# Seven half-size products from the fifth hidden block on, in a float32 SwiGLU FFN pair

## The chip, the cores and the metric

The kernel runs on one core of a Trainium2 chip. The metric is the device time of one execution in microseconds. The engines are named as the profile names them: PE is TensorE (PEld its weight loads), DVE is VectorE, ACT is ScalarE, POOL is GpSimd and SP is SyncE; the last two issue most of the DMA transfers here.

## The reference

One layer of a decoder: a half-step SwiGLU FFN, a token mixer (RWKV-7 heads beside differential attention), and a second half-step FFN, with an RMS norm before and after each. 512 prompt tokens and 8 × 4 sample tokens, 544 in all; model width 1024, hidden width 2816, all float32. The change touches the two FFNs alone.

```python
def swiglu(x, w_in, w_out):
    gate, up = jnp.split(x @ w_in, 2, axis=-1)
    return (jax.nn.silu(gate) * up) @ w_out

def layer(x, l, shift0, wkv0, attend, P):
    g = P['norm_gains'][l]
    h = x + 0.5 * rms_norm(swiglu(rms_norm(x, g[0], NORM_EPS), P['ff1_in'][l], P['ff1_out'][l]), g[1], NORM_EPS)
    m, k, v, wkv, shift = mixer(rms_norm(h, g[2], NORM_EPS), l, shift0, wkv0, attend, P)
    h = h + rms_norm(m, g[3], NORM_EPS)
    h = h + 0.5 * rms_norm(swiglu(rms_norm(h, g[4], NORM_EPS), P['ff2_in'][l], P['ff2_out'][l]), g[5], NORM_EPS)
    return h, k, v, wkv, shift
```

## The kernel before

**Layout.** Activations lie with the features on the 128 partitions and the tokens in the free dimension, in two halves s = 0, 1 of 272 tokens (`HALF`). The width of 1024 is 8 blocks of 128 (`KB`), the hidden width 22 blocks (`FB`).

**Float32 by parts.** Every factor of a matmul is split in two: a high part that ScalarE writes as a rounded copy (`whi`, `xh`, `hd0h`, `sh`), and a low part, the difference (`wlo`, `xl`, `hd0l`, `sl`). A product is three matmuls: high·high, high·low, low·high (L148, L149, L154). `weights` (L112) loads a block of weights, splits it, and makes the low either by a subtraction on VectorE (L124) or, with `added`, as a negated copy on ScalarE (L121) to which a GpSimd transfer adds the weights from memory while it moves them (L122).

**Two kinds of hidden blocks.** A whole block of an FFN multiplies the 8 feature blocks of both token halves with the gate and the up weights: 4 dot products of 24 matmuls, 96 in all. A mixed block, `seven`, takes gate and up as the two rows of a 2 × 2 product with the token halves as its columns, splits the 8 feature blocks in two halves of 4, and computes the four results from seven half-size products of 12 matmuls, 84 in all, with sums and differences before and after. Its left factors are made for each block in `load` and `factors` from the weights: `b` (`raw`, as it is), `b22`, `t1` and `t2`. `t1` is loaded twice from one place by SP (L469), and a GpSimd transfer then adds to it in place (L473); the low of `b` is a negated copy on ScalarE (L494) with an accumulating transfer (L495); `t2` is two additions of VectorE (L497, L498). Its right factors are made once for each FFN in `combined`: `scaled` scales h by the norm in place and splits three of the four quarters (16 steps: L417, and the parts `fa` at L406 on ScalarE and L408 or L410 on VectorE), and `mixtures` overwrites h with four sums or differences of its quarters, 4 tiles each (16 steps: L430, and the parts `sh` and `sl` at L406 and L408). When the last mixture is through, the memory of h is freed, and the pool `wt` with t1, b22 and their parts takes it (L469 and L471 wait for that).

**Groups.** `GROUPS` cuts the 22 blocks into four groups. After each, `products` multiplies the group's hidden tiles (`hd0`, `hd1`) with the output weights: 16 products (8 output blocks u × 2 halves), each of 3 matmuls a hidden block, over the weights of one u at a time. The first group's results are copied from PSUM by ScalarE (L615), those of later groups added by VectorE (L620). The first group is of whole blocks, all later ones of mixed blocks. `scaled` is run in pieces of four steps while blocks 4 and 5 are computed, and `mixtures` two steps with each result of the first group (in `finish`).

**Order.** Within these lines the order of each engine's instructions is set when the program is built, by a scheduler that uses the data's dependences, priorities and `after(...)`, which keeps instructions behind a given one. TensorE's hidden products and the output products of a group run one after the other; in later groups the next mixed block is begun before the output products.

## Time and profile before

| | us |
|---|---|
| median of 3 runs | 1195.4 (1192.81 to 1197.7) |
| profiled execution, its own time | 1202.05 |
| its span | 1200.3 |
| TensorE busy in the span | 1175.4 |
| VectorE busy | 823.3 |
| ScalarE busy | 583.7 |

The granted clock of TensorE was 0.986 over the span. FF1 lies in the first third of the span and FF2 in the last; the mixer stands between them. A line of the timeline reads: start in us from the span's start, duration, engine, line, operation, tile written, tiles read, shape, count, and in brackets the wait before it with what ended it. A matmul's duration there is its way through the pipeline; the pace shows in the starts.

### The profile page before, as it was taken

The page shows a single profiled execution, that of the slowest core. Times are in us where ns is not written, and L with a number is a line of the kernel's source. Part 1 is how long each engine was busy: PE and PEld are TensorE (multiplying, and loading weights), DVE is VectorE, ACT ScalarE, POOL GpSimd, SP SyncE. Part 2 cuts the span into 40 slices and gives each one's busy share as a digit, 9 for nine tenths or more (in the row PEclk, how much of TensorE's full clock was granted, in tenths as well). Part 3 has the DMA queues.
Part 4 walks back from the last instruction along what each step waited for, and adds up shares of the span by engine and source line. Part 5 has one row for each costly group of instructions (what it writes and reads, how often), then busy time and mean ns, then how long its engine had stood idle before and what let it go on. Part 6 is the DMA issues. An engine that isn't in the chain of part 4 may idle for free. (4 is left out here: it accounts for less than half of the span.)

```text
span 1200.3 us, 25442 instructions
## 1 busy us (share of the span) xinstructions
PE 1175.4 (98%) x10020; PEld 1109.7 (92%) x10020; DVE 823.3 (69%) x1878; ACT 583.7 (49%) x1081; POOL 170.9 (14%) x232
## 2 busy tenths in 40 slices
PE   8999999999999999999999999999999999999996
PEld 8999999999999999989887645999999999999995
DVE  7794684865875777768426657888784765857756
ACT  6455552643645664443114535666455634625530
POOL 0001210110101165531000031100002201101001
PEclk9999999999999998899899999999999999999998
DMA  7328885884857456789543468563349876957532
GB/s 257 110 68 239 218 211 122 205 197 120 184 174 201 118 147 182 223 218 256 131 141 104 142 245 297 162 184 124 101 119 243 210 186 152 216 145 183 116 121 75
DMA packets 85833, 205.42 MB, mean 171 GB/s; under 512 B 9144, under 2 KB 20152, under 8 KB 84306
## 3 DMA queue, kind: packets, MB, share of 16 engines
q1 hardware_dynamic: 65378, 148.64, 37.5%
q0 software_dynamic: 18032, 50.70, 23.5%
q10 hardware_dynamic: 2304, 4.46, 1.0%
q8 instruction: 79, 1.29, 0.4%
q14 instruction: 40, 0.33, 0.1%
HBM read 186.12 MB, written 18.95 MB: 171 GB/s over the span
## 5 line engine op out<-in xcount | busy, mean ns | idle before, releaser
L118 ACT ACTIVATE whi<-wraw 128x1024 fp32r<-128x1024 f32 (+2 forms) x127 | 117.0, 924 | 168.9 <-PE mm L149 73.6
L148 PE MATMUL mm<-xh,whi 128*128 128x272 f32 x456 | 122.5, 299 | 3.0 <-ACT whi L645 1.4
L149 PE MATMUL mm<-xl,whi 128*128 128x272 f32 x456 | 121.9, 297 | 0.0
L124 DVE TENSOR_TENSOR wlo<-wraw,whi 128x1024 fp32r<-128x1024 f32 (+2 forms) x100 | 100.6, 1007 | 18.0 <-ACT whi L118 14.0
L148 PEld LDWEIGHTS mm<-xh,whi 128*128 128x128 f32 x456 | 88.7, 195 | 4.7 <-ACT whi L645 1.7
L473 POOL DMA_DIRECT2D t<-in_ff_in_dram x32 | 38.8, 1213 | 362.5 <-DMA t<-in_ff_in_dram 175.9
L149 PEld LDWEIGHTS mm<-xl,whi 128*128 128x128 f32 x456 | 88.9, 195 | 0.5 <-DVE xl L282 0.2
L519 DVE TENSOR_TENSOR ga<-pb,ga 128x272 f32<-128x272 f32 x140 | 61.2, 437 | 23.5 <-PE pb L508 21.2
L154 PE MATMUL mm<-xh,wlo 128*128 128x272 f32 x456 | 69.9, 293 | 0.6 <-DMA wlo<-in_w_in_dram 0.6
L505 PE MATMUL pb<-sh,t1h 128*128 128x272 f32 x256 | 66.7, 288 | 0.0
L620 DVE TENSOR_TENSOR y<-mm,y 128x272 f32<-128x272 f32 x66 | 29.1, 440 | 54.8 <-PE mm L154 54.5
L506 PE MATMUL pb<-sl,t1h 128*128 128x272 f32 x256 | 66.6, 287 | 0.0
L485 ACT ACTIVATE t1h<-t 128x1024 fp32r<-128x1024 f32 x32 | 34.0, 1062 | 61.9 <-issue 37.2
L154 PEld LDWEIGHTS mm<-xh,wlo 128*128 128x128 f32 x456 | 62.5, 192 | 1.5 <-DMA wlo<-in_w_in_dram 1.0
L149 PE MATMUL mm<-hd1l,whi 128*128 128x272 f32 x242 | 62.7, 289 | 1.0 <-DVE hd1l L166 1.0
L149 PE MATMUL mm<-hd0l,whi 128*128 128x272 f32 x242 | 62.6, 288 | 0.0
L148 PE MATMUL mm<-hd0h,whi 128*128 128x272 f32 x242 | 62.2, 288 | 0.0
L148 PE MATMUL mm<-hd1h,whi 128*128 128x272 f32 x242 | 62.1, 289 | 0.0
L148 PE MATMUL pb<-xh,whi 128*128 128x272 f32 x232 | 61.3, 294 | 0.0
L149 PE MATMUL pb<-xl,whi 128*128 128x272 f32 x232 | 60.6, 291 | 0.0
L505 PE MATMUL pb<-fa,whi 128*128 128x272 f32 x216 | 56.2, 288 | 0.0
L506 PE MATMUL pb<-fa,whi 128*128 128x272 f32 x216 | 56.2, 288 | 0.0
(511 smaller groups left out, 3640.5 us busy)
## 6 DMA issues: line engine op xcount, KB each, us to landing
wraw<-in_ff_in_dram SPq DMA_DIRECT2D x55, 512.0 KB, 4.7
wlo<-in_ff_in_dram POOLq DMA_DIRECT2D x34, 512.0 KB, 7.3
t<-in_ff_in_dram SPq DMA_DIRECT2D x64, 256.0 KB, 3.9
t<-in_ff_in_dram POOLq DMA_DIRECT2D x32, 512.0 KB, 5.8
wraw<-in_w_in_dram SPq DMA_DIRECT2D x26, 512.0 KB, 7.9
wlo<-in_w_in_dram POOLq DMA_DIRECT2D x25, 512.0 KB, 8.6
wraw<-in_ff_out_dram SPq DMA_DIRECT2D x32, 384.0 KB, 3.1
wraw<-in_ff_out_dram SPq DMA_DIRECT2D x32, 320.0 KB, 3.4
```

The source lines that it names most:

```text
L118: S.activation(hi, raw, AF.Copy)
L124: V.tensor_tensor(lo, raw, hi.bitcast(FT), op=OP.subtract)
L148: T.matmul(ps, hi, xs[k][0], start=k == 0, stop=False)
L149: latest[0] = T.matmul(ps, hi, xs[k][1], start=False, stop=False).ins
L154: latest[0] = T.matmul(ps, wcols(w, k0 + k)[1], xs[k][0], start=False, stop=k == n - 1).ins
L473: G.dma_start(t1, bass.AP(tensor=src.tensor, offset=src.offset, ap=[[1024, 128], [128 * 1024 + 512, 2], [1, 512]]), accum_op=OP.add)
L485: S.activation(hi, src, AF.Copy)
L505: T.matmul(ps, c, x[k][0], start=k == 0, stop=False)
L506: T.matmul(ps, c, x[k][1], start=False, stop=False)
L519: V.tensor_tensor(dst, p, q, op=op)
L620: V.tensor_tensor(y[s][m], ps, y[s][m], op=OP.add)
```

## The change

- `GROUPS` is (0,4), (4,10), (10,16), (16,22) in place of (0,6), (6,11), (11,16), (16,22): blocks 4 and 5 become mixed blocks, the first group has 4 blocks and the others 6.
- `scaled` runs while blocks 2 and 3 are computed. `mixtures` goes kind by kind, four tiles of each, in place of tile by tile with all four kinds, and every pair of its steps is kept behind the low of the last `split`.
- The first group's output weights have their lows made by VectorE for u = 0 and 1, and by an accumulating transfer (`added`) for the other six.
- In the first mixed block (j = 4) alone, half of t1 is loaded, VectorE makes t1 by two additions and the low of b by a subtraction, and no accumulating transfer is used; and of its seven products t1·s3 and t1·s1 come before t2·s2.

What it moves is seen on two engines and two queues. Names: `h_85` and `h_158` are the two halves of h, `sl_i_n` the low of a mixture, `t_` and `b_` the tiles t1 and b22, `fa` the parts of the scaled quarters. First VectorE in FF1, at the low of a hidden tile of the last whole block (`hd1l`). Before:

```order
L408 TENSOR_TENSOR sl_1_1280<-h_85,sh_1_1279 128x272
L408 TENSOR_TENSOR sl_0_1219<-h_85,sh_0_1218 128x272
L430 TENSOR_TENSOR h_85<-h_85 128x272
L452 TENSOR_TENSOR up<-up,ga 128x272
L408 TENSOR_TENSOR sl_2_1346<-h_85,sh_2_1345 128x272
L430 TENSOR_TENSOR h_85<-h_85 128x272
L408 TENSOR_TENSOR sl_3_1412<-h_85,sh_3_1411 128x272
L408 TENSOR_TENSOR sl_1_1285<-h_85,sh_1_1284 128x272
L408 TENSOR_TENSOR sl_2_1351<-h_85,sh_2_1350 128x272
L166 TENSOR_TENSOR hd1l<-up,hd1h 128x272
L408 TENSOR_TENSOR sl_3_1417<-h_85,sh_3_1416 128x272
```

After:

```order
L410 SCALAR_TENSOR_TENSOR fa<-h_158,fa 128x272 x3
L453 TENSOR_TENSOR up<-up,ga 128x272
L431 TENSOR_TENSOR h_158<-h_158 128x272 x2
L410 SCALAR_TENSOR_TENSOR fa<-h_158,fa 128x272
L431 TENSOR_TENSOR h_158<-h_158 128x272
L166 TENSOR_TENSOR hd1l<-up,hd1h 128x272
L431 TENSOR_TENSOR h_158<-h_85,h_158 128x272 x2
L408 TENSOR_TENSOR sl_0_914<-h_158,sh_0_913 128x272
L431 TENSOR_TENSOR h_158<-h_158 128x272
L408 TENSOR_TENSOR sl_1_919<-h_158,sh_1_918 128x272
L431 TENSOR_TENSOR h_158<-h_85,h_158 128x272
L408 TENSOR_TENSOR sl_2_938<-h_158,sh_2_937 128x272
```

The low stood behind nearly all mixtures, and stands ahead of the lows of all of them now. Next, VectorE at the first mixed block, from the last mixtures on. Before:

```order
L408 TENSOR_TENSOR sl_3_1417<-h_85,sh_3_1416 128x272
L124 TENSOR_TENSOR wlo<-wraw,whi 128x768 x2
L487 TENSOR_TENSOR b22l<-b_1614,b22h 128x512
L124 TENSOR_TENSOR wlo<-wraw,whi 128x768
L487 TENSOR_TENSOR t1l<-t_1611,t1h 128x1024
L124 TENSOR_TENSOR wlo<-wraw,whi 128x768
L497 TENSOR_TENSOR wraw<-t_1611,b_1614 128x512
L498 TENSOR_TENSOR wraw<-wraw 128x512
L487 TENSOR_TENSOR wlo<-wraw,whi 128x1024
L497 TENSOR_TENSOR wraw<-t_1619,b_1622 128x512
```

After:

```order
L408 TENSOR_TENSOR sl_3_1052<-h_85,sh_3_1051 128x272
L408 TENSOR_TENSOR sl_2_1102<-h_85,sh_2_1101 128x272
L408 TENSOR_TENSOR sl_3_1107<-h_85,sh_3_1106 128x272
L501 TENSOR_TENSOR wlo<-wraw,whi 128x1024
L476 TENSOR_TENSOR t_1257<-t_1257,b_1259 128x512
L493 TENSOR_TENSOR b22l<-b_1259,b22h 128x512
L477 TENSOR_TENSOR t_1257<-t_1257,wraw 128x512
L506 TENSOR_TENSOR wraw<-t_1257,b_1259 128x512
L507 TENSOR_TENSOR wraw<-wraw 128x512
L493 TENSOR_TENSOR t1l<-t_1257,t1h 128x1024
L493 TENSOR_TENSOR wlo<-wraw,whi 128x1024
L506 TENSOR_TENSOR wraw<-t_1265,b_1268 128x512
```

The two additions for t1 (L476, L477) and the low of b (L501) are new here, and the four 768-column lows of the output weights are gone from between. GpSimd's queue, from the mixer's tables to the first mixed blocks of FF1; before:

```order
L689 DMA rb_d<-rb_849 128x2560
L473 DMA t_1611<-in_ff_in_dram 128x2x512
L473 DMA t_1619<-in_ff_in_dram 128x2x512
L473 DMA t_1761<-in_ff_in_dram 128x2x512
L495 DMA wlo<-in_ff_in_dram 128x1024
L473 DMA t_1903<-in_ff_in_dram 128x2x512
L495 DMA wlo<-in_ff_in_dram 128x1024 x2
```

After:

```order
L707 DMA rb_d<-rb_569 128x2560
L122 DMA wlo<-in_ff_out_dram 128x512 x6
L479 DMA t_1265<-in_ff_in_dram 128x2x512
L479 DMA t_1406<-in_ff_in_dram 128x2x512
L504 DMA wlo<-in_ff_in_dram 128x1024
L479 DMA t_1548<-in_ff_in_dram 128x2x512
L504 DMA wlo<-in_ff_in_dram 128x1024
```

Six transfers for the output weights' lows stand ahead of the first accumulation of a mixed block, which is now that of the second mixed block. And ScalarE in the first output group, from the first of those lows on; before, in the same group:

```order
L615 ACTIVATE y_0_186<-mm 128x272
L406 ACTIVATE sh_1_1279<-h_85 128x272
L406 ACTIVATE sh_0_1218<-h_85 128x272
L406 ACTIVATE sh_2_1345<-h_85 128x272
L406 ACTIVATE sh_3_1411<-h_85 128x272
L615 ACTIVATE y_1_187<-pb 128x272
L406 ACTIVATE sh_1_1284<-h_85 128x272
L406 ACTIVATE sh_2_1350<-h_85 128x272
L165 ACTIVATE hd1h<-up 128x272
L406 ACTIVATE sh_3_1416<-h_85 128x272
L118 ACTIVATE whi<-wraw 128x768
L615 ACTIVATE y_0_194<-mm 128x272
```

After:

```order
L632 ACTIVATE y_0_194<-pb 128x272
L121 ACTIVATE wlo<-wraw 128x512
L118 ACTIVATE whi<-wraw 128x512
L406 ACTIVATE sh_3_942<-h_158 128x272
L632 ACTIVATE y_1_195<-mm 128x272
L121 ACTIVATE wlo<-wraw 128x512
L406 ACTIVATE sh_2_991<-h_158 128x272
L406 ACTIVATE sh_0_1022<-h_85 128x272
L632 ACTIVATE y_2_196<-mm 128x272
L406 ACTIVATE sh_1_1027<-h_85 128x272
L406 ACTIVATE sh_3_996<-h_158 128x272
L118 ACTIVATE whi<-wraw 128x512
```

Between the mixtures' highs (`sh`, L406) and the results (`y`) there are now the output weights' negated copies (L121).

The diff:

```diff
 FB = DFF // 128
-GROUPS = ((0, 6), (6, 11), (11, 16), (16, 22))
+GROUPS = ((0, 4), (4, 10), (10, 16), (16, 22))
 KH = KB // 2
...
         S.activation(hi, src, AF.Copy)
-        V.tensor_tensor(lo, src, hi.bitcast(FT), op=OP.subtract)
+        made[0] = V.tensor_tensor(lo, src, hi.bitcast(FT), op=OP.subtract).ins
         return hi, lo
...
 
-    turn, last, latest, root = [0], [None], [None], [None]
+    turn, last, latest, root, made = [0], [None], [None], [None], [None]
 
...
 
-    def products(wsrc, x, y, finish, per=1, wx=None, apart=False):
+    def products(wsrc, x, y, finish, per=1, wx=None, apart=False, added=False):
 
...
         for u in range(KB // per):
-            ws.append(weights(wsrc(u), per * n * 128, wx and wx[u // 2]))
+            ws.append(weights(wsrc(u), per * n * 128, wx and wx[u // 2], added and u > 1))
             prod(ws[u], u, 0)
...
         def mixtures():
-            for k in range(KH):
-                a11, a12, a21, a22 = h[0][:, k], h[0][:, KH + k], h[1][:, k], h[1][:, KH + k]
-                for i, (dst, p, q, op) in enumerate(((a22, a22, a21, OP.subtract), (a21, a11, a21, OP.add),
-                                                     (a11, a22, a11, OP.subtract), (a12, a12, a11, OP.add))):
+            for i in range(4):
+                for k in range(KH):
+                    a11, a12, a21, a22 = h[0][:, k], h[0][:, KH + k], h[1][:, k], h[1][:, KH + k]
+                    dst, p, q, op = ((a22, a22, a21, OP.subtract), (a21, a11, a21, OP.add),
+                                     (a11, a22, a11, OP.subtract), (a12, a12, a11, OP.add))[i]
                     V.tensor_tensor(dst, p, q, op=op)
...
             y = [[yp.tile([128, HALF], FT, name=f"y{s}_{m}") for m in range(KB)] for s in range(2)]
-            hid, made = [[], []], [None]
+            hid = [[], []]
             wt = None
...
                 S.activation(g, g, AF.Silu, scale=sign)
-                made[0] = V.tensor_tensor(u, u, g, op=OP.mult).ins
+                V.tensor_tensor(u, u, g, op=OP.mult)
                 hid[s].append(split(hp[s], u, f"hd{s}", bufs=6))
...
                 t1 = wt.tile([128, 2, 512], FT, name="t1", bufs=3)
-                for i in range(2):
+                first = j == GROUPS[0][1]
+                for i in range(1 if first else 2):
                     nc.sync.dma_start(t1[:, i], win[j, 1, :, :512])
...
                 src = win[j, 0]
-                G.dma_start(t1, bass.AP(tensor=src.tensor, offset=src.offset,
-                                        ap=[[1024, 128], [128 * 1024 + 512, 2], [1, 512]]), accum_op=OP.add)
+                if first:
+                    V.tensor_tensor(t1[:, 1], t1[:, 0], b22, op=OP.add)
+                    V.tensor_tensor(t1[:, 0], t1[:, 0], raw[:, :512], op=OP.add)
+                else:
+                    G.dma_start(t1, bass.AP(tensor=src.tensor, offset=src.offset,
+                                            ap=[[1024, 128], [128 * 1024 + 512, 2], [1, 512]]), accum_op=OP.add)
                 loaded[j] = raw, t1, b22
...
                 lo = wp.tile([128, 1024], FR, name="wlo", bufs=4)
-                S.activation(lo, raw, AF.Copy, scale=-1.0)
-                G.dma_start(lo, win[j, 0], accum_op=OP.add)
+                if j == GROUPS[0][1]:
+                    V.tensor_tensor(lo, raw, hi.bitcast(FT), op=OP.subtract)
+                else:
+                    S.activation(lo, raw, AF.Copy, scale=-1.0)
+                    G.dma_start(lo, win[j, 0], accum_op=OP.add)
                 b22w = two(wt, ("b22h", "b22l"), b22, 512)
...
                 yield
-                p = half(acc_tile)
-                product(p, t2, 0, s2)
-                add(u2, p, u2)
+                def doubled():
+                    p = half(acc_tile)
+                    product(p, t2, 0, s2)
+                    add(u2, p, u2)
+
+                if j > GROUPS[0][1]:
+                    doubled()
                 r = half(abank)
                 product(r, t1, 1, s3)
+                if j == GROUPS[0][1]:
+                    q = half(bank)
+                    product(q, t1, 0, s1)
+                    doubled()
                 g1 = add(gu_tile("ga"), r, u2)
-                q = half(bank)
-                product(q, t1, 0, s1)
+                if j > GROUPS[0][1]:
+                    q = half(bank)
+                    product(q, t1, 0, s1)
                 add(u2, q, u2, OP.subtract)
...
                     scaled_raw(0)
-                    behind = [None, None]
-                    for j in range(2, j1, 2):
-                        if midway and j == 4:
-                            midway()
-                        ws = [[weights(win[i, n], 1024, added=begin is None and i == 3) for n in range(2)] for i in (j, j + 1)]
-                        for s in range(2):
-                            for both in ws:
-                                pg, pu = acc_tile(), acc_tile()
-                                for p, w in zip((pg, pu), both):
-                                    dot(p, w, pre.xs[s])
-                                if (j, s) == (2, 0) and both is ws[0]:
-                                    scaled_raw(1)
-                                g, u = gate_up()
-                                V.tensor_tensor(g, pg, pre.rs[s], op=OP.mult)
-                                V.tensor_tensor(u, pu, pre.rs[s], op=OP.mult)
-                                hidden(s, g, u)
-                                with after(j > 2 and behind[0] or None):
-                                    for _ in range(4 * (j > 2)):
-                                        next(scaled, None)
-                                behind.append(made[0])
-                                behind.pop(0)
+                    behind = []
+                    if midway:
+                        midway()
+                    ws = [[weights(win[i, n], 1024, added=begin is None and i == 3) for n in range(2)] for i in (2, 3)]
+                    for s in range(2):
+                        for both in ws:
+                            pg, pu = acc_tile(), acc_tile()
+                            for p, w in zip((pg, pu), both):
+                                dot(p, w, pre.xs[s])
+                            if s == 0 and both is ws[0]:
+                                scaled_raw(1)
+                            g, u = gate_up()
+                            V.tensor_tensor(g, pg, pre.rs[s], op=OP.mult)
+                            V.tensor_tensor(u, pu, pre.rs[s], op=OP.mult)
+                            hidden(s, g, u)
+                            with after(behind[0] if behind else None):
+                                for _ in range(4):
+                                    next(scaled, None)
+                            behind.append(made[0])
+                            del behind[:-1]
                 else:
...
                         S.activation(y[s][m], ps, AF.Copy)
-                        for _ in range(2):
-                            next(mixtures, None)
+                        with after(made[0] if m else None):
+                            for _ in range(2):
+                                next(mixtures, None)
                     else:
...
 
-                products(lambda m: wout[:, m, off:off + n * 128], group, y, finish, wx=late if lastg else None, apart=lastg)
+                products(lambda m: wout[:, m, off:off + n * 128], group, y, finish, wx=late if lastg else None, apart=lastg, added=not gi)
                 off += n * 128
```

## The prediction

> **What bounds the kernel now.** I read the page first, for the share of each engine and the clock; then the chain that ended last, in order of time, for the pace of the seven-product blocks; then TensorE's timeline around the first output group of both FFNs; then the windows of those places, and the rows of VectorE, ScalarE and the DMA queues there.
>
> ```profile
> span 1200.3 us, 25442 instructions
> ...
> PE 1175.4 (98%) x10020; PEld 1109.7 (92%) x10020; DVE 823.3 (69%) x1878; ACT 583.7 (49%) x1081; POOL 170.9 (14%) x232
> ...
> PEclk9999999999999998899899999999999999999998
> ...
> PE 25%; DVE 1%; issue 0%; ACT 0%; DVEq 0%
> ...
> L505 PE MATMUL pb<-sh,t1h 128*128 128x272 f32 x256 | 66.7, 288 | 0.0
> ```
>
> TensorE is busy 98% of the span, its granted clock is at nine tenths or more outside the mixer's slices, and of the 26% of the span that the chain covers it carries 25. So what counts is how many matmuls there are and how often TensorE waits. Their pace is read from starts in time, not from the mean of one (288 ns in the last row, a latency in a pipeline). The chain gives it for one seven-product block of 84 matmuls, from the last product of one block to that of the next:
>
> ```profile
> 1015.91 0.50 PE mm L508 x4
> ...
> 1026.41 0.50 PE mm L508 x4
> ```
>
> 10.50 us for 84 is 0.125 us each. The timeline of TensorE gives the other blocks and the first output group (start, duration, engine, line):
>
> ```profile
> 37.69 0.28 PE L148 MATMUL pb<-xh,whi 128*128 128x272 f32 x1
> ...
> 85.69 0.29 PE L148 MATMUL mm<-hd0h,whi 128*128 128x272 f32 x1
> ...
> 93.11 0.39 PE L148 MATMUL pb<-hd1h,whi 128*128 128x272 f32 x1 [0.24 <-ACT y L615]
> ...
> 95.54 0.39 PE L149 MATMUL mm<-hd1l,whi 128*128 128x272 f32 x1 [0.53 <-DVE hd1l L166]
> ...
> 123.25 0.29 PE L505 MATMUL mm<-fa,whi 128*128 128x272 f32 x1
> ...
> 882.64 0.29 PE L148 MATMUL mm<-hd0h,whi 128*128 128x272 f32 x1
> ...
> 920.19 0.29 PE L505 MATMUL mm<-fa,whi 128*128 128x272 f32 x1
> ```
>
> Blocks 2 to 5 of FF1 take 48.00 us (37.69 to 85.69): 12.0 us for one whole block of 96 matmuls, again 0.125 each. The output group that follows has 16 products of 18 matmuls, 36.0 us at that pace; it takes 37.56 in FF1 and 37.55 in FF2. So 1.56 and 1.55 us are lost there, 0.77 of them as the two waits in brackets. In this stage VectorE is the engine that is full:
>
> ```profile
> 75.00:90.00 15.00, 15.00 (x122) 15.00 (x122) 15.00 (x37) 10.55 (x25) 0.00 (x0) 1.00 0.29 80
> 90.00:105.00 15.00, 14.23 (x111) 13.80 (x111) 10.01 (x22) 7.91 (x16) 2.04 (x2) 1.00 0.73 209
> 105.00:120.00 15.00, 15.00 (x121) 15.00 (x121) 4.20 (x5) 7.77 (x13) 2.52 (x3) 1.00 1.04 268
> ...
> 140.00:150.00 10.00, 10.00 (x82) 10.00 (x81) 8.47 (x16) 6.45 (x10) 1.71 (x3) 1.00 0.92 237
> ```
>
> (Columns: stretch, length, busy time of PE, weight loads, DVE, ACT, POOL, then clock, DMA share, GB/s.) VectorE has 15.00 of 15 us, ScalarE 10.55, DMA 0.29. The DMA is full only one stretch later, when the first mixed blocks are loaded.
>
> **The change part by part.**
>
> 1. *Two blocks per FFN become mixed.* 96 − 84 = 12 matmuls less for each, 1.5 us; two blocks in two FFNs give 4 × 1.5 = **6.0 us**. The output matmuls stay 22 × 16 × 3 in either grouping.
>
> 2. *The first output group shrinks from 18 to 12 matmuls a product*, 24.0 us, and starts two blocks sooner: 85.69 − 24.0 = 61.7 in FF1, 882.64 − 24.0 = 858.6 in FF2. It ends at 85.7 and 882.6, where the first mixed block begins. Of the 3.1 us lost there now (1.56 + 1.55) the cause was VectorE's line of mixtures, which held up the low of the last hidden tile, and ScalarE's sh rows between the evacuations. In the new order that low stands ahead of most mixtures: counted back by VectorE's rows I have it done at 65.4, while TensorE comes to it 38 matmuls into the group, at 61.7 + 4.75 = 66.4. Bounds: none of the 3.1 comes back, or all. I take all, **3.1 us**, and book new waits by themselves.
>
> 3. *Mixtures, in a shorter stage.* What VectorE and ScalarE do there, and what it costs a row:
>
> ```profile
> 78.72 0.44 DVE L430 TENSOR_TENSOR h<-h 128x272 f32<-128x272 f32 x1
> ...
> 82.76 0.79 DVE L430 TENSOR_TENSOR h<-h,h 128x272 f32<-128x272 f32 x2
> ...
> 95.41 0.43 DVE L408 TENSOR_TENSOR sl<-h,sh 128x272 fp32r<-128x272 f32 x1
> ...
> 88.44 1.06 ACT L406 ACTIVATE sh<-h 128x272 fp32r<-128x272 f32 x3
> ...
> 97.05 0.84 ACT L118 ACTIVATE whi<-wraw 128x768 fp32r<-128x768 f32 x1
> 97.78 0.39 ACT L615 ACTIVATE y<-mm 128x272 f32<-128x272 f32 x1
> ...
> 95.87 0.33 SPq L471 DMA_DIRECT2D b<-in_ff_in_dram  x1
> ```
>
> Two VectorE rows in 0.79 with 0.43 for one: a pitch of 0.36. The 32 rows of the mixtures need 11.5 us and were spread over 17 (78.72 to 95.8), with 768-wide lows and others between. The memory of h goes to the pool of t1 and b22 once they are through: b of the first mixed block is issued at 95.87. After, they start near 63.7, have only a handful of other rows among them, and end near 76. Then b, t1 and raw load; the same kind of load lands in about 4 us (rows below), so by 81. Three 512-wide VectorE rows at some 0.6 (an estimate, from 272 columns in 0.36), t1h and t1l (1024 columns, some 1.1 each) bring the first operands to 84 and the low to 85. TensorE comes for them at 85.7 and 87.2. New wait: 0, with about 2 us to spare; the bounds are 0 and, should the loads take 9 us as they do in a full stretch, 3.
>
> That only the first mixed block forms t1 on VectorE takes an accumulating transfer (5.8 us below) out of exactly this chain; the two adds are in the sum above. The new order in that block lets q = t1·s1 run ahead of t2's product, and t2 is ready later than t1 by two adds and a split (about 3 us), covered by r and q (24 × 0.125 = 3.0) and by the two products on b. Cost 0.
>
> 4. *Output lows by transfer, for u above 1.* VectorE loses 6 rows of 512 columns per FFN, ScalarE gains 6, and POOL six transfers of 256 KB that add in flight, ahead of the accumulations of the mixed blocks in its queue. No 256 KB accumulation stands in an FFN before; the nearest rows (page: queue, count, KB, median us to landing), and the landing of the mixed blocks' own lows in the first stretch of FF1 and of FF2:
>
> ```profile
> wlo<-in_ff_in_dram POOLq DMA_DIRECT2D x34, 512.0 KB, 7.3
> t<-in_ff_in_dram SPq DMA_DIRECT2D x64, 256.0 KB, 3.9
> t<-in_ff_in_dram POOLq DMA_DIRECT2D x32, 512.0 KB, 5.8
> ```
> ```profile
> twl<-in_w_in_dram POOLq DMA_DIRECT2D x1, 256.0 KB, 6.0
> ```
> ```profile
> DMA to landing us min/median/max: 7.0/8.9/9.2
> ```
> ```profile
> DMA to landing us min/median/max: 9.4/9.4/9.4
> ```
>
> By the rows ahead of it on ScalarE, the tightest is u = 4 in FF1: issued near 68.5, used 92 matmuls into the group, at 61.7 + 11.5 = 73.2. That leaves 4.7 us. Landing in 3.9 costs nothing; in 6.0, the one 256 KB accumulation of the page, 1.3; in 7.3, 2.6. I take **0.9**, near the 6.0 but with a stage whose DMA share is 0.29. The others have 6 us and more; in FF2 u = 4 has 6.2. [...]
>
> 5. *The second mixed block (j = 5) keeps accumulations for t1 and its low.* Its low is used 1.0 us into the block: 85.7 + 10.5 + 1.0 = 97.2 in FF1, 882.6 + 11.5 = 894.1 in FF2. In ScalarE's order I have the transfer issued at 87.6 and 886.3. The landing rows give 7.0 to 9.4: FF1 has 9.6 us and waits for nothing, FF2 has 7.8 and waits 0 to 1.6. I take **0.8**. Who is queued behind: nothing on POOL but t1 of block 6, which is not needed for 10 us.
>
> 6. *scaled in blocks 2 and 3.* The same 16 rows and 12 splits on VectorE, earlier; the stretch from 60 on has room once the lows of blocks 4 and 5 (eight rows of 1024) are no longer there. 0.
>
> Sum: 6.0 + 3.1 − 0.9 − 0.8 = **7.4 us**. The profiled execution took 1202.05 (span 1200.3), so it would take 1194.65; the median of the runs before, 1195.4, is 6.65 lower, which gives 1188.0. 0.5%, 6.0 us, is about what a measurement of this kernel can tell from no change.
>
> **Rivals.**
>
> *Waits for transfers eat the gain.* The DMA share of 1.04 in 105 to 120 says that the start of the mixed blocks is bound by transfers:
>
> ```profile
> q1 hardware_dynamic: 65378, 148.64, 37.5%
> q0 software_dynamic: 18032, 50.70, 23.5%
> ```
>
> q1 moved 148.64 MB in 37.5% of the span, 330 GB/s; q0 50.70 in 23.5%, 180 GB/s. A mixed block loads 1.25 MB and accumulates 1.05, 3.8 + 5.8 = 9.6 us of the 10.5 that it lasts, so a lag is worked off at about 1 us a block. Should the accumulations of block 5 land in 9.7 instead of 5.8 us after all its covers are used, each FFN waits 3.9: 9.1 − 7.8 = 1.3 us gain, 1194.1. For it: that share. Against: mixed blocks that ran at 0.92 (140 to 150 above) kept TensorE busy for 10.00 of 10 us. Deciding point: a landing over 8 us.
>
> *ScalarE becomes the bound: slower.* In the shortened stage it has 16 sh rows at 0.32, 16 y at 0.28, 11 rows of 512 columns at about 0.53, 7 of 1024 at 0.96 and one or two more: some 22.6 of 24 us, where 10.55 of 15 were used. It works strictly in order, and each sh row waits for the L430 row of VectorE. The one such wait in the trace (of 16 rows):
>
> ```profile
> L406 ACT ACTIVATE sh<-h x16: 412/420/434, 79.7 to 94.1; 128x272 fp32r<-128x272 f32 x16
> ...
>   DVE h L430: 1.8, 1
> ```
>
> 1.8 us over 16 rows is 0.11 each. At 0.28 each (4.55/16) the evacuations of PSUM and with them TensorE are held by all that an FFN gains; at 0.47 the kernel is 0.5% slower; at 0.6, 2 × 9.6 − 9.1 = 10 slower, 1205. For it: mixtures run closer together than before. Against: in the new order four rows of the same kind follow each other on VectorE, so ScalarE finds several ready.
>
> *All of it, and no new wait*, which is what happens if the lows land like the plain loads, in 3.9 us: 9.1, so 1186.3. Against it stands every accumulating row above, none under 5.8.
>
> **How the numbers follow.** Forecast (gain 5 to 9) 0.50; full gain 0.08; transfers eat it 0.30; ScalarE 0.12. The likeliest gives 1188.0. The range goes from the full gain less the spread of the runs (1186.3 − 2.3 = 1184.0) to past the second rival (1196.0); ScalarE's case is left out. Faster by over 0.5% (below 1189.4): the full gain and most of the forecast, plus little else, 0.55; within: 0.34; slower: 0.11.
>
> **What would show it.** Right: the pace of 0.125 unchanged; first output group near 24 us in both FFNs; 21 us for blocks 4 and 5; TensorE's waits for hd1l and y gone, new ones of under 1 us for wlo. Wrong: TensorE waiting for y or mm behind ScalarE (third case), for wlo, t1h or t1l of blocks 4 and 5 for over 2 us (second), or for something outside both FFNs that the earlier end of FF1 uncovers, on which I put nothing: the mixer's own waits start from FF1's end and should move with it.

## The result, and the profile after

The changed kernel is slower: 1205.81 us median of 6 runs (1202.3 to 1208.9) against 1193.99 of 6 runs of the kernel before on the same chip; ratio 1.0087, 95% interval 1.0063 to 1.0111. The medians are 11.8 us apart, by the ratio it is some 10.4 us. The forecast was 1188.0. Its profiled execution took 1206.4 us (span 1204.6).

The same lines of the page as of before:

```profile
span 1204.6 us, 25450 instructions
...
PE 1171.4 (97%) x9972; PEld 1105.1 (92%) x9972; DVE 828.7 (69%) x1896; ACT 593.1 (49%) x1107; POOL 184.2 (15%) x248
...
PEclk8999999999999999899799999999999999999998
```

48 matmuls are gone, as counted, but the span is not shorter: TensorE stands still 8.3 us longer than in the trace of before (33.2 against 24.9). Its list of waits (what waits, for what, total us, times, longest) names some of that, and three of the rows are of a kind that the list of before did not have or had smaller:

```profile
PE mm L517 <- DMA wlo<-in_ff_in_dram: 3.5, 1, 3.5
...
PE pb L996 <- issue: 1.9, 1, 1.9
...
PE mm L148 <- ACT hd0h L165: 1.0, 1, 1.0
```

The first is the low of a mixed block in FF2, the second is in the mixer, far from the change, the third is at the second output group of FF1. Which stretch holds how much is read from TensorE's timeline, from the first and last output product of each FFN:

```profile
62.23 0.29 PE L148 MATMUL mm<-hd0h,whi 128*128 128x272 f32 x1
...
388.84 0.91 PE L154 MATMUL mm<-hd1h,wlo 128*128 128x272 f32 x6
...
860.16 0.29 PE L148 MATMUL pb<-hd0h,whi 128*128 128x272 f32 x1
...
1189.22 0.91 PE L154 MATMUL pb<-hd1h,wlo 128*128 128x272 f32 x6
```

A control of the kernel before, traced with the experiments, has the same points:

```profile
85.61 0.29 PE L148 MATMUL mm<-hd0h,whi 128*128 128x272 f32 x1
...
388.32 0.91 PE L154 MATMUL mm<-hd1h,wlo 128*128 128x272 f32 x6
...
875.88 0.29 PE L148 MATMUL mm<-hd0h,whi 128*128 128x272 f32 x1
...
1178.60 0.91 PE L154 MATMUL mm<-hd1h,wlo 128*128 128x272 f32 x6
```

In the kernel before, the first output product comes two whole blocks (24.0 us) later in the program; put at the same place (24.0 off the two first products of before), the stretches compare in the table. FF1 and FF2 are from there to the last output product; the stretch between them holds the mixer and the first four blocks of FF2.

| us | start to FF1's products | FF1 | between | FF2 |
|---|---|---|---|---|
| before, trace of the forecast (1202.05) | 61.69 | 326.71 | 470.24 | 326.71 |
| before, control (span 1193.9) | 61.61 | 326.71 | 463.56 | 326.72 |
| after | 62.23 | 326.61 | 471.32 | 329.06 |

Against the control: 0.6 at the start, −0.1 in FF1, **+7.8 between the FFNs**, +2.3 in FF2, in sum 10.6, close to the difference of the runs. The stretch between is split by a matmul that both traces have at the beginning of FF2; the control and the changed kernel:

```profile
823.76 0.39 PE L129 MATMUL mm<-xh,whi 128*128 128x272 f32 x1 [0.48 <-ACT ga L560]
```
```profile
830.98 0.39 PE L129 MATMUL pb<-xh,whi 128*128 128x272 f32 x1 [0.48 <-ACT ga L578]
...
841.72 1.27 PE L154 MATMUL pb<-xh,wlo 128*128 128x272 f32 x8 [0.79 <-DMA wlo<-in_ff_in_dram]
```

To that matmul it is 435.44 us from FF1's last output product in the control and 442.14 in the changed kernel: **6.7 us are lost in the mixer**, where the change changes nothing. The other 1.1 are in the first four blocks of FF2, 0.8 of them as a wait for a low that before does not wait for; why was not tried. Inside the FFNs the expected gain of some 4 us each does not appear.

### The profile page after: what moved, and what is told of

Read it like the earlier page. It is cut to its first block, busy times and chain, and to the rows that moved or that the text cites. A ratio compares the mean times of both kernels' runs of the same rounds, so it can differ in the third digit from the quotient of the medians.

```text
span 1204.6 us, 25450 instructions
## 1 busy us (share of the span) xinstructions
PE 1171.4 (97%) x9972; PEld 1105.1 (92%) x9972; DVE 828.7 (69%) x1896; ACT 593.1 (49%) x1107; POOL 184.2 (15%) x248
## 4 chain that ended last, share of the span: by engine, by line
PE 74%; DMA 10%; DVE 7%; issue 4%; ACT 2%; SPq 1%; POOL 1%; DVEq 0%; POOLq 0%; ACTq 0%
PE mm L154 8%; PE mm L148 8%; PE mm L149 8%; PE pb L514 5%; PE pb L515 5%; PE pb L517 5%; PE pb L154 4%; PE pb L148 4%; PE pb L149 4%; DMA b<-in_ff_in_dram 3%; PE mm L517 2%; PE mm L515 2%; PE mm L514 2%; DMA t<-in_ff_in_dram 1%; DMA wlo<-in_ff_in_dram 1%
## 5 line engine op out<-in xcount | busy, mean ns | idle before, releaser
L148 PE MATMUL mm<-xh,whi 128*128 128x272 f32 x376 | 101.2, 298 | 3.1 <-ACT whi L663 1.7
L149 PE MATMUL mm<-xl,whi 128*128 128x272 f32 x376 | 100.4, 296 | 0.0
L124 DVE TENSOR_TENSOR wlo<-wraw,whi 128x768 fp32r<-128x768 f32 (+2 forms) x80 | 82.6, 1034 | 15.2 <-ACT whi L118 11.5
L148 PEld LDWEIGHTS mm<-xh,whi 128*128 128x128 f32 x376 | 72.7, 194 | 4.7 <-ACT whi L663 1.9
L149 PEld LDWEIGHTS mm<-xl,whi 128*128 128x128 f32 x376 | 72.7, 194 | 0.7 <-DVE xl L282 0.2
L514 PE MATMUL pb<-fa,whi 128*128 128x272 f32 x236 | 61.5, 288 | 0.0
L515 PE MATMUL pb<-fa,whi 128*128 128x272 f32 x236 | 61.4, 288 | 0.0
L504 POOL DMA_DIRECT2D wlo<-in_ff_in_dram x34 | 37.0, 1087 | 158.1 <-ACT wlo L503 156.4
L491 ACT ACTIVATE whi<-wraw 128x1024 fp32r<-128x1024 f32 x36 | 38.2, 1062 | 42.5 <-DVE wraw L507 25.3
L506 DVE TENSOR_TENSOR wraw<-t,b 128x512 f32<-128x512 f32 x36 | 24.9, 692 | 49.3 <-DMA b<-in_ff_in_dram 30.5
L154 PE MATMUL mm<-xh,wlo 128*128 128x272 f32 x376 | 58.1, 295 | 0.0
```

The source lines that it names most:

```text
L124: V.tensor_tensor(lo, raw, hi.bitcast(FT), op=OP.subtract)
L148: T.matmul(ps, hi, xs[k][0], start=k == 0, stop=False)
L149: latest[0] = T.matmul(ps, hi, xs[k][1], start=False, stop=False).ins
L154: latest[0] = T.matmul(ps, wcols(w, k0 + k)[1], xs[k][0], start=False, stop=k == n - 1).ins
L491: S.activation(hi, src, AF.Copy)
L504: G.dma_start(lo, win[j, 0], accum_op=OP.add)
```

## Experiments

Each kernel ran against the kernel before on the same chip; the rounds ran on different chips, so kernels of different rounds compare best by their ratios to before. Two theories were kept apart throughout: one for the FFNs (late transfers at the first mixed blocks), one for the mixer (the place at which TensorE fetches its instructions).

**Control.** The kernel before, unchanged.

> The kernel before, unchanged, as a control with a trace of its own: the trace used for the forecast took 1202.05 us, the runs 1191.9 to 1197.7. If the missing 4 to 8 us lie in one place, a trace that takes about 1194 shows it. If they lie in the FFNs, the pace of 0.125 us a matmul or the 1.56 us lost in the first output group must come out smaller; if they lie in the mixer, its stretch between the last output product of FF1 and the first block of FF2 (438.8 us in both traces so far) must be about 431. The second is expected, since the FFNs of before have nearly nothing to lose.

1195.67 us, ratio 1.0002 (0.9987 to 1.0016). FFNs to 0.01 us as in the first trace; the mixer's stretch, between the same two matmuls, is 432.1 us in place of 438.8 (393.82 to 825.96). So the first trace of before had itself lost 6.7 us in the mixer. The windows of before, of the control and of the changed kernel at that place (clock in the third column from the end):

```profile
584.00:586.00 2.00, 2.00 (x29) 1.71 (x28) 0.65 (x2) 0.15 (x2) 0.00 (x0) 0.50 0.08 24
```
```profile
575.00:595.00 20.00, 19.94 (x308) 17.46 (x306) 7.56 (x14) 3.82 (x10) 0.00 (x0) 1.00 0.54 156
```
```profile
575.00:595.00 20.00, 18.11 (x220) 16.04 (x220) 5.46 (x9) 1.72 (x4) 0.00 (x0) 0.66 0.25 68
```

In the same 20 us the control runs 308 matmuls at full clock and the changed kernel 220 at 0.66: a wait of 1.9 us, then some 13 us at a granted clock of 0.50. The first trace of before has the half clock too, for some 10 us, after a shorter wait. That place accounts for about 5 of its 6.7 us; some 2 more were lost earlier, most of them at 461 to 468, where its granted clock was 0.50 to 0.51 until 467.

**Where the instructions come from.** In both kernels the wait falls into one run of 56 small matmuls (L978 of before, L996 of after). TensorE's timeline of the control, of the first trace of before, and of the changed kernel:

```profile
578.32 1.32 PE L978 MATMUL pb<-ld,tmp 32*32 32x32 f32 x56
```
```profile
580.80 0.44 PE L978 MATMUL pb<-ld,tmp 32*32 32x32 f32 x16
...
581.96 0.82 PE L978 MATMUL pb<-ld,tmp 32*32 32x32 f32 x40 [0.72 <-issue]
```
```profile
577.66 0.78 PE L996 MATMUL pb<-ld,tmp 32*32 32x32 f32 x37
...
580.33 0.74 PE L996 MATMUL pb<-ld,tmp 32*32 32x32 f32 x19 [1.89 <-issue]
```

The break lies after 16 of the 56 in before and after 37 in after, 21 deeper; FF1 has 24 matmuls fewer ahead of it. The instruction queue q8 of before (page: packets, MB, share):

```profile
q8 instruction: 79, 1.29, 0.4%
```

That is 16 KB a packet. If these packets hold TensorE's instructions alone (an estimate: 12 of them come in 200 to 400 of before, for 1604 matmuls, and 16 in 600 to 800, for 2074), 10020 matmuls with as many weight loads in 79 packets are 127 matmuls a packet. While TensorE stands still one such packet is under way (the transfers from 578 to 580 of the changed kernel):

```profile
q8 instruction: 1, 0.02, 3.0%
```

If the break is the border of a packet, matmuls added anywhere ahead move it. The edit adds 12 of one column to the warm-up at the very start, which the trace counts as 24 (9996 in place of 9972):

```diff
-    for _ in range(10):
-        T.matmul(ps[:, :128], ones, ones, start=True, stop=True)
+    for _n in [128] * 10 + [1] * 12:
+        T.matmul(ps[:, :_n], ones, ones[:, :_n], start=True, stop=True)
```

> The changed kernel with 12 matmuls of one column added right behind the 10 warm-up matmuls at the very start (24 matmuls as the trace counts them, as many as FF1 lost by the change), nothing else. The traces show TensorE standing still for 1.8 to 2.0 us in the middle of a run of 56 small matmuls in the mixer (released by nothing that the profile shows, one 16 KB packet of the instruction queue arriving meanwhile), then a granted clock of 0.50 for some 13 us. Theory A (place of the instruction fetch): the change takes 24 matmuls out of TensorE's program ahead of that point, which moves the border of the fetched packets 21 to 24 matmuls deeper into the run; putting 24 in at the start moves it back: no stall, no drop of the clock, and 6 to 7 us less, about 1199. Theory B (the mixer is slowed by when its transfers run, or by chance): no change, about 1205.

1200.69 us, ratio 1.0054 (1.0034 to 1.0073), by the ratios some 4 us less, with intervals that overlap; the run of 56 is whole again and the stretch between the FFNs is 466.5 in place of 471.3. That is 4.8 us less where 6 to 7 were expected. The stall is gone, but in this trace the clock still falls to 0.50 behind the run, for some 7 us (the control takes 0.88 us for the same 42 matmuls):

```profile
583.94 1.38 PE L996 MATMUL pb<-ld,tmp 32*32 32x32 f32 x42
```
```profile
583.00:590.00 7.00, 7.00 (x68) 6.60 (x68) 2.60 (x5) 0.60 (x1) 0.00 (x0) 0.51 0.01 2
```

So the stall is not the only way into the half clock there. The reverse, 52 of them (104 counted) in the kernel before:

> The kernel before with 52 matmuls of one column added at the start (104 as the trace counts them, which with 128 to a packet moves the borders 24 forward, to where the changed kernel has them); the FFNs are untouched. They may delay the first block by up to 5 us, which the trace shows by the start of block 1's matmuls. Theory A: the stall of 1.8 us and the clock of 0.50 appear in the mixer's run of 56, and the stretch from FF1's last output product to FF2 grows by 6 to 7 us. Theory B: that stretch stays at the 487.6 us of the control (to the first output product of FF2).

1219.34 us, ratio 1.0201 (1.0175 to 1.0227). 15.1 us of it are the padding at the start (first output product at 100.69 in place of 85.61), three times the 5 us that were allowed for it, and say nothing of the mixer. The mixer's own stretch does: the break stands after 40 of 56, and the stretch between the FFNs is 470.0 (493.96 less 24.0) in place of 463.6.

```profile
591.27 0.82 PE L978 MATMUL pb<-ld,tmp 32*32 32x32 f32 x40
594.22 0.44 PE L978 MATMUL pb<-ld,tmp 32*32 32x32 f32 x16 [2.13 <-issue]
```

So the stall goes with the place of the break, in a kernel whose FFNs are untouched: 0.72 us after 16 of 56 (none in the control), 2.13 after 40. Theory A holds in both directions. The place moves as the count says: 16 becomes 40 with 104 matmuls more (24 short of 128, which 9972 matmuls in the changed kernel's 78 packets give), and 37 becomes 13 with 24 more, where two of the padded kernels below show a short wait (0.35 and 0.41 us). What is shown is the place; that it is a packet's border is inferred from these moves. That the packet is late because the DMA engines are full there (share 0.90 to 0.92 in 575 to 580 with and without the stall) is not, since nothing was taken off them; nor is it shown why before has the same border 21 matmuls earlier and mostly gets through, nor why it is 21 and not 24.

**The low of the second mixed block.**

```diff
-                if j == GROUPS[0][1]:
+                if j <= GROUPS[0][1] + 1:
                     V.tensor_tensor(lo, raw, hi.bitcast(FT), op=OP.subtract)
```

> The changed kernel with the low of the second mixed block (j = 5) made by VectorE as in the first, not by an accumulating transfer. Theory A (the low that lands late is what TensorE waits for): the waits of 3.5 us (FF2) and 0.6 us (FF1) on it go, and 3 to 4 us come back against the changed kernel: about 1202. Theory B (the loads of b22 and t1 are late as such, the low is only the last of a row of late operands): another operand of blocks 4 to 6 is waited for instead, and less than 1.5 us comes back.

1202.75 us, ratio 1.0053 (1.003 to 1.0076). FF1 325.82 and FF2 325.88, that is 0.8 and 3.2 less than in the changed kernel: theory A. That 4.0 us come back where the two waits measured 4.1 is partly luck: behind FF2's wait the clock had been 0.50 for some 3.4 us, which cost 1.7 us more and goes as well, and new waits of 0.3 to 0.6 us (for t1l and for the low of block 6) and a longer one for hd0h take as much away. The changed kernel behind its wait:

```profile
900.00:903.00 3.00, 3.00 (x15) 3.00 (x16) 2.08 (x5) 2.07 (x4) 0.00 (x0) 0.54 1.09 275
```

With the padding as well:

> The low of the second mixed block by VectorE and the 12 added matmuls at the start. Theory A: 1202.75 without the padding minus 6 to 7, about 1196, as fast as the kernel before or up to 2 us faster, and with a spread of runs as narrow as before's. Theory B: about 1203.

**1192.83 us, ratio 0.998 (0.9966 to 0.9995)**: faster than both kernels, by a little. From 1202.75 to this only the padding differs: 9.9 us in the medians, 8.7 by the ratios, whose intervals lie clear of each other; the granted clock over the span is 0.989 to 0.994 in its 12 runs and 0.981 to 0.989 in the 12 without the padding. The stretches between the FFNs differ by 7.2 us in the two traces (465.56 against 472.74). At the place in the mixer it does in 20 us nearly what the control does, with a break after 13 of the 56:

```profile
577.63 0.40 PE L996 MATMUL pb<-ld,tmp 32*32 32x32 f32 x13
578.38 0.88 PE L996 MATMUL pb<-ld,tmp 32*32 32x32 f32 x43 [0.35 <-issue]
```
```profile
575.00:595.00 20.00, 19.65 (x304) 17.08 (x303) 7.16 (x13) 3.61 (x9) 0.00 (x0) 1.00 0.53 158
```

**The output weights' lows.** `added=False` for the first group: all lows by VectorE.

> The changed kernel with all lows of the first group's output weights made by VectorE (no accumulating transfer in that group; six more rows of 512 columns on VectorE, six fewer on ScalarE in each FFN). Theory A (these transfers crowd the stage): the waits of 0.24 and 0.49 us on them go and the loads of b22 of the first mixed block, 7.5 us in FF2, land in 4 to 5, which takes 2 or more off the 3.5 us wait: in all 3 us better, about 1203. Theory B (VectorE is the scarce engine there): VectorE's mixtures end about 4 us later, h is freed later, and the first mixed block waits: 2 us or more slower than the changed kernel.

1203.47 us, ratio 1.0061 (1.0038 to 1.0084). The total is what theory A said, but its interval overlaps that of the changed kernel, and the FFNs give only 1.1 us of it: FF1 327.19, FF2 327.41, 0.6 more and 1.7 less. The first output group of FF1 does become clean (24.21 us in place of 25.46) and the wait for hd0h in the second one goes, but the lows of block 5 are waited for 2.7 us in FF1, where it was 0.6, and 3.0 in FF2. In FF1 that is theory B: VectorE's last low of the mixtures ends 3.8 us later, counted from the first output product, and the low of block 5 is issued 2.0 later. In FF2 b22 lands in 4.5 us in place of 7.4, as theory A said, and the low of block 5 is issued 1.1 earlier, but it takes 11.4 us to land in place of 9.9. Neither theory covers that. With the low of block 5 by VectorE too:

> Both edits: low of the second mixed block and all output lows by VectorE. If transfers are the whole loss inside the FFNs, 5 to 6 us better than the changed kernel, about 1200; if VectorE becomes the bound of the shortened stage, slower than the edit on the second block's low alone.

1204.27 us, ratio 1.0063 (1.0033 to 1.0093): FF1 330.91 (TensorE waits 5.5 us for the low of block 6, the first accumulated one now), FF2 323.96. In FF1 the loss moves to the next accumulated operand; in FF2 it does not appear, and 2.8 of the 3.7 us that the forecast gives each FFN are there. Together the FFNs are 3.2 us longer than with the low of block 5 alone, the second forecast by its sign, though the intervals of the runs overlap.

**Undoing the aids**, each with the padding, so that the mixer's stall stays out (p1 is the padded changed kernel above, FF1 325.69, FF2 329.53). The old order of the mixtures:

> The padded changed kernel with the mixtures in the order of before (tile by tile, all four kinds, and not held behind a low of the hidden tiles). Theory A (the new order pays): the low of the last hidden tile again stands behind mixtures, TensorE waits for it in the first output group (0.5 us or more in each FFN), that group is 1 us or more longer, and the four quarters end no earlier, so that nothing is won back in the first mixed blocks. Theory B (what the first mixed blocks wait for is transfers, whatever the order): the FFNs are within 1 us of the padded changed kernel's 325.7 and 329.5 (first output product to last).

1199.6 us, ratio 1.0044 (1.0029 to 1.0058): FF1 327.22, FF2 328.75, 1.5 more and 0.8 less, no wait for hd1l in either group. Theory B, nearly: the order of the mixtures decides little for the sum. The waits change place all the same: in FF2 TensorE waits 2.4 us for a low of the output weights, and 1.0 in place of 3.4 for the low of block 5. No special first mixed block:

```diff
-                first = j == GROUPS[0][1]
+                first = False
```
(and the usual order of products and the usual low for that block.)

> The padded changed kernel without the special first mixed block: t1 of block 4 is loaded twice and added to by an accumulating transfer, the low of its b is one too, and its products stand in the usual order. Theory A (an accumulating transfer takes 5.8 to 9.7 us where a load and an addition take 5 to 8): t1 and the low of block 4 are late by 3 to 6 us and the low of block 5, behind them in the queue, by as much: 3 to 8 us more in each FFN. Theory B (one transfer more in a full stretch, one less on VectorE): within 2 us.

1208.67 us, ratio 1.0109 (1.0087 to 1.0131): FF1 329.81, FF2 334.39, 4.1 and 4.9 more. TensorE waits for t1, the operand that the special block takes out of the accumulating queue:

```profile
PE pb L514 <- ACT t1h L491: 8.2, 2, 4.8
```

Theory A. And the groups alone, without any of the three aids:

> The padded changed kernel with the groups alone: old order of the mixtures, no special first mixed block, all output lows by VectorE. If the three aids work as such, each FFN is at least as slow as the worse of the two kernels before it, 333 us or more from the first output product to the last; if the aids only move the waits, it is within 2 us of the padded changed kernel.

1205.86 us, ratio 1.0086 (1.0064 to 1.0108): FF1 332.52, FF2 332.08, 6.8 and 2.6 more than padded. That is more than the 2 us of waits that only move, but short of the 333 expected of aids that add up, and against the kernel without the special block alone FF1 is 2.7 longer and FF2 2.3 shorter: the aids pay together, and their effects do not add.

**Two tries at more.** Raw weights of blocks 5 and 6 loaded behind b22 of block 4:

```diff
-                nc.sync.dma_start(raw, win[j, 0])
+                with after(lead_b[0] if j > GROUPS[0][1] else None):
+                    nc.sync.dma_start(raw, win[j, 0])
```

> As the second, and in addition the loads of the plain weights (raw) of blocks 5 and 6 stand behind b22 of block 4 on SP's queue, where they stood ahead of it. If the late b22 of block 4 (7.5 us to landing) is what delays the first mixed blocks, it lands in 4 to 5 us, and each FFN is 0.5 to 1.5 us shorter than in the second kernel: about 1194. If the DMA engines are simply full there, the same bytes come in another order, another operand is late, and the time stays within 0.5 us of the second.

1193.4 us, ratio 0.9988 (0.9973 to 1.0003): FF1 325.55 and FF2 325.35 against 325.01 and 326.72 of the second kernel, which is the one with the low of block 5 by VectorE and the padding. In FF2 b22 lands in 5.9 us in place of 8.2, in the first output group of FF1 the longest wait for a low of the output weights grows from 0.5 to 1.8. The same bytes in another order, the same time. And the composite:

> A version meant to beat both: low of the second mixed block by VectorE, output lows by accumulating transfers only for u = 2, 3, 5, 6 (u = 4 and 7 are waited for 0.2 and 0.6 us in FF1), and the 12 more warm-up matmuls bought by making all 22 of them 58 columns wide, so that the start costs nothing. Against 1192.8 of the second kernel with padding: 0.7 us from the start and 0.5 to 1 us from the first output groups, minus up to 1 us for two more rows on VectorE: about 1191.5, and a ratio to before of 0.997.

1195.61 us, ratio 1.0 (0.9981 to 1.0019): FF1 326.02, FF2 326.73; the FFNs together are no shorter (652.75 against 651.73 of the second kernel), and the wider warm-up did not make the start shorter (first output product at 63.28 against 62.32). It missed.

## Why the prediction was wrong

*The pace and the count (6.0 us): right.* 48 matmuls fewer, and where nothing waits the stretches are what 0.125 us a matmul makes them: from the second group's products to the third's, 36 + 63 = 99.0 us by count, 99.26 measured in FF1 of the kernel with VectorE's output lows.

*The first output group (3.1 us back, 0.9 for u = 4): half right.* The waits for hd1l and for y are gone, but the new order of the mixtures, to which I put it, was not needed for that: with the old order in the new groups the wait for hd1l is gone too. The new ones are on two lows of the output weights in FF1, the last of which (u = 7) I had called safe:

```profile
74.24 0.78 PE L154 MATMUL mm<-hd0h,wlo 128*128 128x272 f32 x4 [0.24 <-DMA wlo<-in_ff_out_dram]
...
85.57 0.78 PE L154 MATMUL mm<-hd0h,wlo 128*128 128x272 f32 x4 [0.49 <-DMA wlo<-in_ff_out_dram]
```

The group lasts 25.46 us in FF1 and 24.53 in FF2 against 24.0: 2.0 lost where I booked 0.9. The transfers landed in 4.1 to 7.7 us; my rows had 3.9 to 7.3.

*Step 3, the first mixed block's operands ("by 81", 0 us): wrong in FF2.* The mixtures ended within about a microsecond of what I said (FF2: last low at 875.17, b22 issued at 875.70). But b22 was taken at the "about 4 us" of the page's medians, though the 9 us of a full stretch were named beside it. It landed in 5.1 us in FF1 and in 7.4 in FF2. TensorE did not wait for block 4 even so; the delay shows one block later. FF2, ahead of the first mixed block: three raw loads of 512 KB are issued first on SP, b22 lands late, and the rows behind it on VectorE (which waits 5.57 us for it) and ScalarE (2.76) pass the delay on to block 5. On ScalarE even a result's copy that does not need b22 is held: the copies, 1.5 us apart until 880.03, go on at 883.73, behind the high of b22 at 883.19, though the next product was through at 881.5.

```profile
868.75 6.42 SPq L467 DMA_DIRECT2D wraw<-in_ff_in_dram  x3
...
875.70 0.42 SPq L473 DMA_DIRECT2D b<-in_ff_in_dram  x1
```
```profile
883.20 0.69 DVE L476 TENSOR_TENSOR t<-t,b 128x512 f32<-128x512 f32 x1 [5.57 <-DMA b<-in_ff_in_dram]
```
```profile
888.55 1.04 ACT L503 ACTIVATE wlo<-wraw 128x1024 fp32r<-128x1024 f32 x1
```
```profile
889.89 0.89 POOL L504 DMA_DIRECT2D wlo<-in_ff_in_dram  x1 [1.62 <-ACT ga L535]
```
```profile
899.82 0.94 PE L517 MATMUL mm<-fa,wlo 128*128 128x272 f32 x4 [3.47 <-DMA wlo<-in_ff_in_dram]
```

*Step 5, the low of block 5 (0.8 us): mis-sized, 3.5 in FF2 and 0.6 in FF1, and in FF2 1.7 more by the half clock behind the wait.* Counted from the first output product, I had it issued at 27.7 us in FF2 and 25.9 in FF1, landing 7.0 to 9.4 later and used at 35.5. It was issued at 29.7 and 27.2, landed 9.9 and 10.6 later, and TensorE was there at 36.2 and 37.2. So both the issue and the landing were late. The chain just shown makes the issue late in FF2, but it is not the whole cause: with all output lows by VectorE, b22 landed in 4.5 us, the low was issued at 28.7 and still waited for 3.0, with 11.4 us to landing. The operand was the right one, and the rival "waits for transfers eat the gain" is what came true inside the FFNs (its price of 3.9 us, at a landing of 9.7, is near the wait in FF2).

*Waits that no step named*: 0.8 us in the first blocks of FF2, shown above, where step 6 booked nothing; and at the start of the second output group TensorE waits 1.05 us in FF1 and 0.54 in FF2 for hd0h of the block just finished.

```profile
158.51 0.39 PE L148 MATMUL mm<-hd0h,whi 128*128 128x272 f32 x1 [1.05 <-ACT hd0h L165]
```

It is there in some variants and not in others (FF1 of five is without it), and its cause was not tried apart.

*ScalarE as the bound*, the rival that forecast a slower kernel: not seen. No wait of TensorE for y stands in the list of after; that this rival had the sign right is luck.

*The mixer ("the mixer's own waits start from FF1's end and should move with it", nothing booked): the step that failed, with step 5.* 6.7 of the 10.6 us lie there. Taking 24 matmuls out of FF1 moved the break in the mixer's run from 16 of 56 to 37, and the wait at it grew from 0.72 us (none in the control) to 1.89. Part of the price stood in the trace beforehand: I took the 6.65 us between the profiled execution and the median as a level and subtracted it, where about 5 of it were one place, a wait of 0.72 us and a clock of 0.50 behind it. A median that is 0.55% below the trace is a finding to explain and not a constant to carry over. The forecast went from the median, without that loss; the traces of the changed kernel and of its three variants without padding all have the wait, of 1.8 to 2.0 us.

By size: forecast −7.4, measured +10.6 in the traces. Of the 18.0 between, 6.7 are the mixer, 0.6 the start and 10.7 the FFNs: some 5 for the low of block 5 with the clock behind it, 1.6 for hd0h, 1.1 each for the first output groups and for the first blocks of FF2, and some 2 that no listed wait shows.

## What to carry to other kernels

Before summing gains, ask why the traced execution differs from the median, and find the places. When instructions leave an engine's program, look downstream for a stretch of many tiny instructions: here its stall depended on where the break fell (1.89 us after 37 of 56, 2.13 after 40, 0.35 after 13), and twelve cheap matmuls at the start shifted it. That the DMA was busy there (share 0.90 in 575 to 580) may be needed too; it was not tried. Where operands come from a full DMA stretch, count from landing times of that stretch and of the loads issued ahead, not from the page's medians (in FF2 of the changed kernel b22 took 7.4 us where its median is 4.5, the low of block 5 9.9 where it is 7.3), and follow the delay through the rows behind it on VectorE and ScalarE to the next block.

## What the runs showed of the hardware

**The clock.** In the run of small matmuls a wait of 0.72 us (first trace of before) was followed by some 10 us at a granted clock of 0.50 (584 to 594), one of 1.89 us (the changed kernel) by some 13, though TensorE was busy again at once. Behind 2.13 us (the shifted kernel before) the clock was 0.52 in 595 to 600. Behind 1.78 us (low of block 5 by VectorE, without padding) eight matmuls a few rows on (L1032) took 2.08 us, against 1.16 for the same eight in the control (L1014). Waits of 0.35 and 0.41 us there (padded: low of block 5 by VectorE, and the groups alone) were followed by a clock of 1.00. The padded changed kernel has 7 us of the half clock there without any wait, and before and after have it in 486 to 490 too (0.50, TensorE busy for 2.00 of every 2 us), so a wait that the profile shows is not needed.

In the FFNs the five waits of 2.37 to 4.85 us in the table began at the full clock (a pace of 0.125 us a matmul), and each had a stretch at 0.22 to 0.23 us a matmul behind it.

| kernel | wait, us | at |
|---|---|---|
| changed | 3.47 | 899.82 |
| padded, old order of the mixtures | 2.37 | 868.13 |
| padded, no special first mixed block | 3.38 | 92.11 |
| padded, no special first mixed block | 4.85 | 890.61 |
| padded, groups alone | 3.05 | 886.73 |

Behind the first the clock was 0.50 in 901 to 903. Waits of 1.30 us (old order) and 1.53 (no special block) in FF2 were followed by the pace of 0.125 us; so was one of 1.42 us for kbs in the mixer.

**Instruction packets.** Queue q8 moved 79 packets of 16 KB in before and 78 in the changed kernel. TensorE's list of waits in the changed kernel has one row that ends in no releaser ("issue"), 1.9 us once, the one beside which a packet was under way. It cost 1.9 us, and with the clock behind it some 7 us, by the two kernels that differ in the padding alone (7.2 us between the FFNs).
